# The w_down sums issued one step per store ahead of the FFN, and two modulation rows computed under the projections

## The chip, the cores and the metric

The kernel runs on one core of one Trainium2 chip. A core has a matrix engine (PE), a vector engine (DVE), an activation engine (ACT), a general engine (POOL), and a queue engine (SP) that mostly issues DMAs; POOL issues DMAs too. Each engine works through its own instructions strictly in order, and an instruction that waits for a semaphore holds everything behind it on that engine. The metric is the device time in microseconds (us) of one execution. Changes of this kernel under about 1% can't be told from no change.

## The reference

One layer of a hybrid block over 1024 tokens of width 1024, one sample, with 256 context tokens. Cut to what matters here:

```python
sh1, sc1, ga1, sh2, sc2, ga2 = split(silu(c) @ w_mod + b_mod)           # six modulation rows of 1024
hx = rmsnorm(x, g_pre_mix) * (1 + sc1) + sh1
u_pool, u_lru, u_gate, g_pool, g_lru = split(hx @ w_in)
y_pool = pool_mixer(u_pool)                    # 2D window means, grouped matmul
h_f, h_b = two RG-LRU scans over u_lru         # causal conv, gates, linear scan both ways
y_lru = (h_f + h_b) * gelu(u_gate)
m = sigmoid(g_pool) * (y_pool @ w_proj_pool) + sigmoid(g_lru) * (y_lru @ w_proj_lru)
x = x + ga1 * rmsnorm(m @ w_out, g_post_mix)
h = rmsnorm(x, g_pre_ffn) * (1 + sc2) + sh2
g, u = split(h @ w_up)                         # 2 x 3072 columns
f = (gelu(dwconv3x3(g)) * u) @ w_down
out = x + ga2 * rmsnorm(f, g_post_ffn)
```

## The kernel before, in words

Everything is in float32, but each matmul operand is split into a high and a low part in fp32r, and a product is three matmuls (high x high, high x low, low x high). So every weight tile of 128 x 1024 that comes from memory takes three steps, in `load_w` (L91): SP issues the load into a tile with the tag `raw`, ACT casts it to the high part (L89 CAST) and DVE subtracts for the low part (L89 TENSOR_TENSOR). The tag `raw` has three buffers for the whole kernel, given out in turn; who asks for the fourth waits until the first has been read. A unit of 48 matmuls of 128 x 512 (`unit_mm`, L228) makes 128 channels of a projection.

The stages, in order: a start (norm, the modulation of the first norm, up to about 100 us); z1 (to about 285 us: pooling, the gelu of the LRU's gate, gate units); z2, the LRU stage (to about 590 us: per channel block c one `lru_in` unit, four gate matmul groups, two scans on DVE, and a gate unit); pj, the projections (to 800 us: gate units that are left, `pp_unit` for y_pool, `pl_unit` for y_lru, and under them `form_pair`, which prepares three FFN weight sets and stores them in memory, and the loads of w_out); the w_out matmuls with the second norm (to 911 us); the FFN's up part (24 steps f, to 1401 us); the down part (to 1640 us).

The FFN and its down part use Strassen-like products, for which sums of blocks of w_down are needed. `sum_steps` (L850) forms them with accumulating DMAs on POOL's queue in a 128 x 2048 tile `n2raw` and stores them in `sd_d`: 12 blocks p of 5 steps, 60 steps of one to three DMAs, each step waiting for the one before it. They are issued three steps per f in the FFN loop (L972), chained behind the store of `gu_d` (L917).

The four later modulation rows (ga1, sh2, sc2, ga2) are computed by `mod_steps` (L252). For each row j there are eight loads `rawm` of w_mod, each with one DVE instruction that adds into `acc` (L264, L266); then four matmuls with a matrix of ones (`pm`, L270) that sum over partitions; then two row instructions on DVE (L273 with a row loaded into `rowb`, and for j=0, 2, 3 a second one, L275 to L279); then a store into `row_d`. `rawm` and `rowb` are both of the tag `raw`. Rows 0 and 1 are computed in z1, where weights are loaded three units ahead (L411); rows 2 and 3 in z2, three steps per channel block (L541). In pj and z2, `load_w` stands in the unit that uses the weight.

Tile tags in pj: `bc0` to `bc2` and `mq` are shared by stages, gate outputs and the pieces of `form_pair` (`piece`, L609, a ring of five). In the down part `finish` (L1029) loads a tile `xr` of x1 (two buffers), scales, adds and stores it; it is called for the second half of the tokens at product q=5 and for the first half at q=6, the last product.

The order on each engine comes from a scheduler: program order unless a `high_priority` offset or `issue_after` moves it.

Of the kernel before, what the change touches and what calls it, by code (L numbers as in the profile page):

```python
# [40 lines left out]
def block_kernel(ctx: ExitStack, tc: tile.TileContext, x, cx, vecs, rowv, icnt, w_mod1, w_mod, w_in, pool_w,  # L41
# [58 lines left out]
    n2raw = gpool.tile([P, 4, 512], F32, name="n2raw", tag="n2raw")  # L100
    epsc = cpool.tile([P, 1], F32, name="epsc")
# [150 lines left out]
    def mod_steps(zp, pp, rng, nbuf):  # L252
# [4 lines left out]
        for j in rng:  # L257
            acc = zp.tile([P, D], F32, name=uid("acc"), tag="acc", bufs=1)
# [9 lines left out]
            ps = pp.tile([P, SEQ], F32, name=uid("pm"), tag="pu", bufs=nbuf)  # L268
# [18 lines left out]
    with tc.tile_pool(name="z1", bufs=1, reuse_waits="tile") as zp:  # L287
        n_unit = [0]
        mods = mod_steps(zp, pp, (0, 1), 3)
# [3 lines left out]
        def gate_unit(which, c):  # L293
# [5 lines left out]
            G.dma_start(sg_d[c, :, which, :], s)  # L299
# [57 lines left out]
        def ug_unit(c):  # L357
# [6 lines left out]
            G.dma_start(gl_d[c], gl)  # L364
            return mm

        def pool_out(g, o, after):
# [16 lines left out]
            G.dma_start(yp_d[c], yp)  # L384
# [69 lines left out]
    with tc.tile_pool(name="z2", bufs=1, reuse_waits="tile") as zp, \  # L454
# [3 lines left out]
        def gate_unit(which, c):  # L458
# [6 lines left out]
            G.dma_start(sg_d[c, :, which, :], s)  # L465
# [22 lines left out]
        def lru_scan(c, xp, xc, wg):  # L488
# [46 lines left out]
            G.dma_start(yl_d[c], y)  # L535
# [18 lines left out]
    with tc.tile_pool(name="pj", bufs=1, reuse_waits="tile") as zp:  # L554
# [14 lines left out]
        for j, (which, c) in enumerate(gq):  # L569
# [5 lines left out]
            G.dma_start(sg_d[c, :, which, :], s)  # L575
# [20 lines left out]
        def pl_unit(c):  # L596
# [7 lines left out]
            G.dma_start(m_d[c], s)  # L604
# [4 lines left out]
        def piece():  # L609
            n_pc[0] += 1  # L610
            i = n_pc[0] % 5
# [41 lines left out]

        h2 = H("h2")
# [98 lines left out]
    with tc.tile_pool(name="ff", bufs=1, reuse_waits="tile") as zp:  # L753
# [96 lines left out]
        def sum_steps(p):  # L850
            n2v = n2raw.rearrange("p (g h) c -> p g h c", g=2)
            lo, up = w_down[p * P:(p + 1) * P, :], w_down[(NH + p) * P:(NH + p + 1) * P, :]
            hv = lambda a: a.rearrange("p (h c) -> p h c", h=2)
            add = lambda dst, src: G.dma_start(dst, src, accum_op=ALU.add)  # L854
            yield G.dma_start(n2v[:, 0], hv(lo)), G.dma_start(n2v[:, 1], hv(up))
            yield (add(n2v[:, 1], hv(lo)), add(n2v[:, 0, 0, :], lo[:, 512:1024]),
                   add(n2v[:, 0, 1, :], lo[:, 0:512]))
            yield add(n2v[:, 1, 0, :], lo[:, 512:1024]), add(n2v[:, 0, 0, :], up[:, 512:1024])
            yield add(n2v[:, 1, 0, :], up[:, 512:1024]),
# [299 lines left out]
```

## Time and profile before

| what | value |
|---|---|
| median of 3 runs | 1640.2 us (1632.53 to 1645.49) |
| the profiled execution's own time | 1641.79 us |
| span of the profiled execution | 1640.0 us |
| PE busy | 1568.3 us, 96% of the span |
| DVE busy | 1210.5 us, 74% |
| ACT busy | 687.0 us, 42% |
| POOL busy | 239.3 us, 15% |
| bytes moved by DMA | 289.15 MB, 176 GB/s over the span |

PE is busy nearly all the time, so the profile is read by looking for the places where PE stands idle and for what it waits there, and by asking for each stage how close another resource (a DMA, the three `raw` buffers, DVE) is to making PE wait. The view of stretches gives the busy time of each engine between two times, the clock that PE was granted (1.00 is full speed), the mean busy share of the DMA engines and the rate. In the view in order of time, "[3.79 <-ACT i L504]" says that the engine was idle for 3.79 us before the instruction and that an instruction of ACT, of line 504, ended it.

### The profile page before, as it was taken

How to read it: one execution, taken by the hardware profiler on the slowest of the kernel's cores; microseconds unless marked ns; L12 is line 12 of the kernel's file. 1: busy time of each engine (PE TensorE's matmuls, PEld its weight loads, DVE VectorE, ACT ScalarE, POOL GpSimd, SP SyncE). 2: the span in 40 equal slices, each digit the busy share in tenths (PEclk: the TensorE clock that was granted, in tenths of full speed). 3: DMA queues.
4: the chain of work that ended last, by engine and by line, in shares of the span. 5: the costliest groups of instructions: out<-in, count | busy, mean ns of one | idle time of the engine just before them, and what ended most of it. 6: DMA issues, size and time to landing. Idle time of an engine off the chain costs nothing.

```text
span 1640.0 us, 18320 instructions
## 1 busy us (share of the span) xinstructions
PE 1568.3 (96%) x6976; PEld 1265.2 (77%) x6976; DVE 1210.5 (74%) x1368; ACT 687.0 (42%) x828; POOL 239.3 (15%) x328
## 2 busy tenths in 40 slices
PE   6899999999999999999999989999899999999997
PEld 4588888877778788888788768877677777888885
DVE  7777664787887654354378889998798889787567
ACT  8523322565567734122143334333333334445442
POOL 1400200111112211010110122222222220000000
PEclk9999999999999999999999999999999999999999
DMA  8335454324233266399344567777667673687555
GB/s 314 114 103 165 138 184 139 127 97 148 84 103 116 90 232 230 124 289 300 131 141 142 209 195 186 193 199 197 176 183 180 178 187 110 217 320 256 175 188 192
DMA packets 98358, 289.15 MB, mean 176 GB/s; under 512 B 10871, under 2 KB 10999, under 8 KB 97502
## 3 DMA queue, kind: packets, MB, share of 16 engines
q1 hardware_dynamic: 60926, 170.64, 31.7%
q0 software_dynamic: 37344, 117.34, 24.2%
q8 instruction: 54, 0.88, 0.2%
q14 instruction: 34, 0.28, 0.1%
HBM read 221.34 MB, written 66.60 MB: 176 GB/s over the span
## 4 chain that ended last, share of the span: by engine, by line
PE 32%; DVE 10%; DMA 6%; ACT 2%; issue 2%; SPq 0%; DVEq 0%; ACTq 0%
PE pb L740 7%; PE pb L1017 6%; PE pb L706 5%; PE pc L740 4%; DMA raw<-in_w_up_dram 4%; PE pd L1017 4%; DVE gc L900 4%; PE pd L740 3%; PE pc L1017 2%; DVE wf L89 1%; DMA out_dram<-xr 1%; ACT wf L89 1%; DVE raw L801 0%; DMA xr<-x_d 0%; DVE w L89 0%
## 5 line engine op out<-in xcount | busy, mean ns | idle before, releaser
L242 PE MATMUL pu<-hx,whl 128*128 128x512 f32 x1056 | 266.7, 392 | 1.4 <-DVE whl L89 1.4
L900 DVE SCALAR_TENSOR_TENSOR gc<-gc,vec 128x945 f32<-128x945 f32 (+1 forms) x192 | 234.2, 1220 | 4.7 <-ACT gc L886 1.8
L89 ACT CAST whl<-raw 128x1024 fp32r<-128x1024 f32 (+1 forms) x109 | 109.1, 1003 | 305.8 <-DMA raw<-in_w_up_dram 74.4
L242 PEld LDWEIGHTS pu<-hx,whl 128*128 128x128 f32 x1056 | 186.8, 188 | 39.5 <-DVE whl L89 2.0
L89 DVE TENSOR_TENSOR whl<-raw,whl 128x1024 fp32r<-128x1024 f32 (+1 forms) x109 | 128.0, 1177 | 93.7 <-ACT whl L89 93.4
L242 PE MATMUL pg<-hx,whl 128*128 128x512 f32 x480 | 117.1, 396 | 0.0
L740 PE MATMUL pb<-h,wf 128*128 128x512 f32 x384 | 96.3, 400 | 11.3 <-ACT fk L810 11.3
L242 PEld LDWEIGHTS pg<-hx,whl 128*128 128x128 f32 x480 | 89.5, 191 | 19.3
L740 PEld LDWEIGHTS pb<-h,wf 128*128 128x128 f32 x384 | 71.8, 191 | 31.5 <-ACT fk L810 16.9
L740 PE MATMUL pb<-h,whl 128*128 128x512 f32 x384 | 94.9, 393 | 0.0
L706 PE MATMUL pb<-whl,mH 128*128 128x512 f32 x384 | 89.1, 392 | 1.0 <-ACT mH L700 1.0
L242 PE MATMUL pb<-hy,whl 128*128 128x512 f32 x384 | 87.8, 389 | 0.0
L706 PEld LDWEIGHTS pb<-whl,mH 128*128 128x128 f32 x384 | 71.5, 188 | 16.6 <-ACT mH L700 1.5
L740 PEld LDWEIGHTS pb<-h,whl 128*128 128x128 f32 x384 | 71.2, 188 | 16.9 <-ACT fk L810 2.5
L242 PEld LDWEIGHTS pb<-hy,whl 128*128 128x128 f32 x384 | 72.1, 188 | 14.9
L854 POOL DMA_DIRECT2D n2raw<-in_w_down_dram x72 | 63.0, 1006 | 122.9 <-DMA n2raw<-in_w_down_dram 122.6
L740 PE MATMUL pc<-nf,wf 128*128 128x512 f32 x288 | 72.9, 402 | 6.3 <-DVE gc L875 6.2
L1017 PE MATMUL pb<-hD 128*128 128x512 f32 x306 | 78.0, 390 | 0.0
L740 PEld LDWEIGHTS pc<-nf,wf 128*128 128x128 f32 x288 | 53.6, 190 | 22.5 <-DVE gc L875 11.5
L740 PE MATMUL pc<-nf,w 128*128 128x512 f32 x288 | 70.0, 391 | 0.2 <-DVE gc L847 0.2
L498 PE MATMUL pg<-xp,whl 128*128 128x512 f32 x192 | 61.3, 416 | 7.7 <-ACT i L504 7.6
L1017 PEld LDWEIGHTS pb<-hD 128*128 128x128 f32 x306 | 57.3, 188 | 12.3 <-DVE CA L1042 0.3
(319 smaller groups left out, 2986.9 us busy)
## 6 DMA issues: line engine op xcount, KB each, us to landing
raw<-in_w_up_dram SPq DMA_DIRECT2D x41, 512.0 KB, 4.6
raw<-in_w_in_dram SPq DMA_DIRECT2D x40, 512.0 KB, 4.7
n2raw<-in_w_down_dram POOLq DMA_DIRECT2D x36, 512.0 KB, 6.0
rawm<-in_w_mod_dram SPq DMA_DIRECT2D x32, 512.0 KB, 4.1
n2raw<-in_w_down_dram POOLq DMA_DIRECT2D x60, 256.0 KB, 5.7
rw<-gu_d SPq DMA_DIRECT2D x58, 256.0 KB, 5.1
gu_d<-gc POOLq DMA_DIRECT2D x24, 512.0 KB, 3.2
sd_d<-n2raw POOLq DMA_DIRECT2D x24, 512.0 KB, 4.6
```

Of the source, the lines that this page charges most:

```text
L89: return A.copy(hi, src), V.tensor_sub(lo, src, f32(hi))
L242: mm = T.matmul(ps[:, h * 512:(h + 1) * 512], wv[:, wi, k, :], act(h, k, ai), start=st, stop=sp)
L498: T.matmul(pg[:, h * 512:(h + 1) * 512], wg[:, wi, m, :], xp[:, ai, h * 512:(h + 1) * 512], start=(i == 0), stop=(i == 2))
L706: mm = T.matmul(ps[:, h * 512:(h + 1) * 512], mh[ai][:, k, :], wo[k][:, wi, h * 512:(h + 1) * 512], start=(k == 0 and i == 0), stop=(k == ...
L740: mm = T.matmul(ps, w(wi, j), b(ai, j), start=(start and j == 0 and i == 0), stop=(j == 3 and i == 2), skip_group_check=True)
L854: add = lambda dst, src: G.dma_start(dst, src, accum_op=ALU.add)
L900: V.scalar_tensor_tensor(o, gv[:, r0 + dr:r1 + dr, c0 + dc:c1 + dc], cw(i, j), o, op0=ALU.mult, op1=ALU.add)
L1017: T.matmul(bank[dst](t), op[:, gi, 512 + t * P:512 + (t + 1) * P], op[:, wi, H0], start=(first and p == 0 and i == 0), stop=(p == NH - 1 a ...
```

## The change

Three edits.

- `sum_steps` moves to the start of the kernel with a helper `sum_step`. One step is issued behind each store that POOL issues in z1 (18), z2 (16) and pj (11, the last behind `m_d` of c=4): 45 of the 60 steps, nine blocks p. The other 15 are issued one per f in the FFN, for f=2 to 16.
- Modulation rows 2 and 3 are computed in pj, three steps behind each `pl_unit` c=0 to 5, and no longer in z2. `acc` uses the tag `bc2`, so `piece` has a ring of four; the matmuls' result has the bank "c" of the projections.
- The four x1 tiles of the first half of the tokens are loaded at q=5 into the dead tile `N`, not in `finish`.

```diff
+    def sum_step(after, limit=45):
+        if n_step[0] >= limit:
+            return after
+        with tc.issue_after(after.ins):
+            i = next(dsteps[n_step[0]])[-1]
+        n_step[0] += 1
+        return i
...
-            G.dma_start(sg_d[c, :, which, :], s)
+            sum_step(G.dma_start(sg_d[c, :, which, :], s))
...
         gq = [(0, c) for c in range(6)] + [(1, c) for c in range(KT)]
-        mods = mod_steps(zp, pp, (2, 3), 2)
         cur = lru_in(0)
         for c in range(KT):
-            some(mods, 3)
             nxt = lru_in(c + 1) if c + 1 < KT else None
...
         def piece():
             n_pc[0] += 1
-            i = n_pc[0] % 5
+            i = n_pc[0] % 4
...
+        mods = mod_steps(lambda: zp.tile([P, D], F32, name=uid("acc"), tag="bc2"), lambda: pbank("c"), (2, 3))
         for c in range(KT):
             m_last = pl_unit(c)
+            some(mods, 3)
             if 2 <= c < 2 + NPF:
                 form_pair(c - 2)
...
-            for _ in range(3):
-                g = next(steps, None)
-                if g is not None:
-                    with tc.issue_after(chain[-1].ins):
-                        chain.append(next(g)[-1])
+            if f > 1:
+                chain.append(sum_step(chain[-1], 60))
...
+            xr = N[:, 0, 2 * t:2 * t + 2, :] if h == 0 else zp.tile([P, 2, 512], F32, name=uid("xr"), tag="xr", bufs=2)
+            if h:
+                load_x(xr, tt)
...
+            if q == 5:
+                for t in range(4):
+                    load_x(N[:, 0, 2 * t:2 * t + 2, :], t)
```

On PE, at the end of the projections, before: `pd`, `pc` with `yps` are the `pp_unit`s (six matmuls per input block), `pb` with `hy` the `pl_unit`s. Here is the `pl_unit` of c=2 with what follows it.

```order
L242 MATMUL pb_4909<-hy,whl_4906 128x512 x48
L242 MATMUL pc_4996<-yps_3967,whl_4993 128x512 x6
L242 MATMUL pc_4996<-yps_3972,whl_4993 128x512 x6
...
L242 MATMUL pb_5197<-hy,whl_5194 128x512 x48
L242 MATMUL pb_5304<-hy,whl_5301 128x512 x48
L242 MATMUL pb_5383<-hy,whl_5380 128x512 x48
```

And after, at the same place, with `pc_5003` and `pc_5436` the sums over partitions of rows 2 and 3.

```order
L265 MATMUL pb_4943<-hy,whl_4940 128x512 x48
L293 MATMUL pc_5003<-acc_4741,ones 128x512 x2
L265 MATMUL pc_5048<-yps_4025,whl_5045 128x512 x6
...
L265 MATMUL pb_5378<-hy,whl_5375 128x512 x48
L293 MATMUL pc_5436<-acc_5158,ones 128x512 x2
L265 MATMUL pb_5473<-hy,whl_5470 128x512 x48
```

The row sum now stands behind `pl_unit` c=2 (`pb_4943`) and ahead of `pp_unit` c=6 (`pc_5048`), and the second one between `pl_unit`s c=5 and c=6.

On SP, the loads around `pl_unit` c=2 before: the two FFN weight tiles of the first `form_pair`, then the weights of `pp_unit` c=6 and `pl_unit` c=3.

```order
L618 DMA raw584_4961<-in_w_up_dram 128x1024
L619 DMA raw585_4962<-in_w_up_dram 128x1024
L585 DMA sgp568_4729<-sg_d_78 128x1024
L585 DMA sgp572_4786<-sg_d_78 128x1024
L94 DMA raw592_4991<-in_w_pp_dram 128x1024
L94 DMA raw596_5048<-in_w_pl_dram 128x1024
```

After, the same place, and then the place around `pl_unit` c=5 (`raw642_5468` is the weight of `pl_unit` c=6). All tiles named `raw`, `rawm` and `rowb` share the three buffers.

```order
L284 DMA rawm567_4997<-in_w_mod_dram 128x1024
L284 DMA rawm568_5000<-in_w_mod_dram 128x1024
L278 DMA rowb570_5006<-in_rowv_dram 1x1024
L278 DMA rowb571_5009<-in_rowv_dram 1x1024
L607 DMA sgp548_4751<-sg_d_78 128x1024
L607 DMA sgp552_4808<-sg_d_78 128x1024
L640 DMA raw572_5013<-in_w_up_dram 128x1024
L607 DMA sgp559_4879<-sg_d_78 128x1024
L607 DMA sgp563_4936<-sg_d_78 128x1024
L607 DMA sgp579_5041<-sg_d_78 128x1024
L641 DMA raw573_5014<-in_w_up_dram 128x1024
L94 DMA raw580_5043<-in_w_pp_dram 128x1024
```

```order
L278 DMA rowb631_5439<-in_rowv_dram 1x1024
L278 DMA rowb632_5442<-in_rowv_dram 1x1024
L94 DMA raw633_5446<-in_w_out_dram 128x1024
L607 DMA sgp641_5466<-sg_d_78 128x1024
L94 DMA raw635_5451<-in_w_out_dram 128x1024
L607 DMA sgp645_5525<-sg_d_78 128x1024
L94 DMA raw637_5456<-in_w_out_dram 128x1024
L94 DMA raw639_5461<-in_w_out_dram 128x1024
L94 DMA raw642_5468<-in_w_pl_dram 128x1024
```

Two `rowb` loads now take two of the three buffers ahead of `raw573_5014` and `raw580_5043`; in the second place they stand ahead of three w_out loads and of `raw642_5468`. The second `rowb` (`rowb571_5009`) and `raw580_5043` have the same buffer, and so do `raw635_5451` and `raw642_5468`.

On POOL, in the FFN, before, and then after: `gu_d` is the store of a finished f, `n2raw` and `sd_d` are the sums.

```order
L917 DMA gu_d_6389<-gc806_6629 128x1024
L854 DMA n2raw_86<-in_w_down_dram 128x1024
L854 DMA n2raw_86<-in_w_down_dram 128x512 x5
L917 DMA gu_d_6389<-gc815_6748 128x1024
L860 DMA sd_d_85<-n2raw_86 128x1024 x2
L855 DMA n2raw_86<-in_w_down_dram 128x1024 x2
L854 DMA n2raw_86<-in_w_down_dram 128x512 x2
```

```order
L929 DMA gu_d_6479<-gc806_6707 128x1024
L106 DMA n2raw_86<-in_w_down_dram 128x1024 x2
L929 DMA gu_d_6479<-gc815_6822 128x1024
L105 DMA n2raw_86<-in_w_down_dram 128x1024
L105 DMA n2raw_86<-in_w_down_dram 128x512 x2
L929 DMA gu_d_6479<-gc824_6949 128x1024
```

Between two stores of `gu_d` there were three steps, and there is one.

## Rows read from the trace of the kernel before

**Rows 1.** Stretches: length, busy us (instructions) by engine, PE clock, DMA share, GB/s.

```profile
300.00:400.00 100.00, 95.34 (x443) 77.08 (x442) 78.69 (x68) 64.12 (x64) 15.21 (x10) 0.97 0.34 108
400.00:500.00 100.00, 95.59 (x446) 76.88 (x445) 84.92 (x70) 62.64 (x62) 19.78 (x13) 0.98 0.35 113
...
900.00:1000.00 100.00, 89.45 (x372) 69.91 (x371) 86.47 (x96) 36.12 (x45) 18.55 (x29) 0.97 0.63 192
1000.00:1100.00 100.00, 99.80 (x434) 79.98 (x433) 94.87 (x99) 37.89 (x45) 25.67 (x36) 1.00 0.77 204
1100.00:1200.00 100.00, 93.44 (x393) 74.12 (x392) 83.69 (x88) 36.86 (x45) 23.22 (x33) 0.97 0.68 182
```

**Rows 2.** Longest wait of PE, 300 to 560 us (total us, times, longest).

```profile
PE pg L498 <- ACT i L504: 7.6, 2, 3.8
```

**Rows 3.** In order of time, ACT, LRU stage (start, length; idle before).

```profile
385.90 1.04 ACT L89 CAST whl<-raw 128x1024 fp32r<-128x1024 f32 x1 [4.22 <-DMA raw<-in_w_in_dram]
```

**Rows 4.** In order of time, SP, LRU stage.

```profile
363.63 0.33 SPq L94 DMA_DIRECT2D raw<-in_w_in_dram  x1
364.88 11.72 SPq L261 DMA_DIRECT2D rawm<-in_w_mod_dram  x3
...
379.61 0.33 SPq L94 DMA_DIRECT2D raw<-in_w_in_dram  x1
```

**Rows 5.** Longest waits of PE in the FFN (total us, times, longest).

```profile
PE pb L740 <- ACT fk L810: 11.3, 8, 2.8
PE pd L740 <- ACT fk L810: 6.2, 2, 5.2
```

**Rows 6.** Longest wait of ACT in the FFN.

```profile
ACT whl L89 <- DMA raw<-in_w_up_dram: 68.6, 18, 11.1
```

**Rows 7.** The chain that ended last, one transfer in the FFN (start, length).

```profile
1156.28 8.49 DMA raw<-in_w_up_dram
```

**Rows 8.** In order of time, ACT, FFN.

```profile
1164.84 1.04 ACT L89 CAST whl<-raw 128x1024 fp32r<-128x1024 f32 x1 [11.09 <-DMA raw<-in_w_up_dram]
```

**Rows 9.** In order of time, DVE, end.

```profile
1629.96 1.28 DVE L1049 SCALAR_TENSOR_TENSOR xr<-CA,rs,xr 128x1024 f32<-128x1024 f32 x1 [2.34 <-DMA xr<-x_d]
1631.16 0.68 DVE L1042 TENSOR_TENSOR CA<-pc,CA 128x512 f32<-128x512 f32 x1
...
1635.55 1.42 DVE L1049 SCALAR_TENSOR_TENSOR xr<-CA,rs,xr 128x512 f32<-128x512 f32 x2 [0.94 <-DMA xr<-x_d]
```

**Rows 10.** Projections by stretches, PE alone: length, busy, clock, DMA share, GB/s.

```profile
562.00:690.00 128.00, 128.00 (x567) 1.00 0.53 185
690.00:740.00 50.00, 50.00 (x222) 1.00 0.92 293
```

**Rows 11.** In order of time, PE, a row sum in the LRU stage, a unit of the projections.

```profile
358.59 1.88 PE L270 MATMUL pm<-acc,ones 128*128 128x512 f32 x4
...
722.79 11.04 PE L242 MATMUL pc<-yps,whl 128*128 128x512 f32 x48
```

**Rows 12.** In order of time, DVE, row instructions of row 2 in z2.

```profile
362.40 1.21 DVE L273 TENSOR_TENSOR acc<-pm,rowb 1x1024 f32<-1x1024 f32 x1
363.64 1.21 DVE L277 SCALAR_TENSOR_TENSOR acc<-acc,rowb 1x1024 f32<-1x1024 f32 x1
```

**Rows 13.** Groups of DVE and ACT in the projections (busy, mean ns).

```profile
L89 DVE TENSOR_TENSOR whl<-raw,whl 128x1024 fp32r<-128x1024 f32 x28 | 34.2, 1221 | 30.5 <-ACT whl L89 30.4
...
L602 DVE SCALAR_TENSOR_TENSOR sgp<-sgp,pb 128x1024 f32<-128x1024 f32 x7 | 8.5, 1220 | 39.6 <-PE pb L242 32.6 <-DMA sgp<-sg_d 7.0
```

**Rows 14.** The same view, ACT.

```profile
L89 ACT CAST whl<-raw 128x1024 fp32r<-128x1024 f32 x28 | 29.4, 1051 | 78.1 <-PE pb L242 30.4 <-PE pd L242 22.4 <-DMA raw<-in_w_out_dram 12.7
```

**Rows 15.** DMA issues, 600 to 690 us: count, KB, median us to landing.

```profile
raw<-in_w_pp_dram SPq DMA_DIRECT2D x5, 512.0 KB, 4.0
```

**Rows 16.** DMA issues, 690 to 740 us.

```profile
raw<-in_w_pp_dram SPq DMA_DIRECT2D x2, 512.0 KB, 7.5
```

More of the change, by code (lines that the diff above doesn't have):

```diff
@@ L100, in block_kernel, with sum_steps @@
     n2raw = gpool.tile([P, 4, 512], F32, name="n2raw", tag="n2raw")
+    def sum_steps(p):
+        n2v = n2raw.rearrange("p (g h) c -> p g h c", g=2)
+        lo, up = w_down[p * P:(p + 1) * P, :], w_down[(NH + p) * P:(NH + p + 1) * P, :]
+        hv = lambda a: a.rearrange("p (h c) -> p h c", h=2)
+        add = lambda dst, src: G.dma_start(dst, src, accum_op=ALU.add)
+        yield G.dma_start(n2v[:, 0], hv(lo)), G.dma_start(n2v[:, 1], hv(up))
+        yield (add(n2v[:, 1], hv(lo)), add(n2v[:, 0, 0, :], lo[:, 512:1024]),
+               add(n2v[:, 0, 1, :], lo[:, 0:512]))
+        yield add(n2v[:, 1, 0, :], lo[:, 512:1024]), add(n2v[:, 0, 0, :], up[:, 512:1024])
+        yield add(n2v[:, 1, 0, :], up[:, 512:1024]),
+        yield tuple(G.dma_start(sd_d[p, i], n2v[:, i].rearrange("p h c -> p (h c)")) for i in range(2))
+    dsteps = [st_ for p in range(NH) for st_ in [sum_steps(p)] * 5]
+    n_step = [0]
+    def sum_step(after, limit=45):
[5 more added lines that the diff above has]
+        return i
     epsc = cpool.tile([P, 1], F32, name="epsc")
@@ L257, in mod_steps @@
         for j in rng:
-            acc = zp.tile([P, D], F32, name=uid("acc"), tag="acc", bufs=1)
+            acc = new_acc()
             for k in range(KT):
@@ L267, in mod_steps @@
                 yield
-            ps = pp.tile([P, SEQ], F32, name=uid("pm"), tag="pu", bufs=nbuf)
+            ps = new_ps()
             for h in range(2):
@@ L288, in block_kernel @@
         n_unit = [0]
-        mods = mod_steps(zp, pp, (0, 1), 3)
+        mods = mod_steps(lambda: zp.tile([P, D], F32, name=uid("acc"), tag="acc", bufs=1),
+                         lambda: pp.tile([P, SEQ], F32, name=uid("pm"), tag="pu", bufs=3), (0, 1))
         wload = lambda u: wq.pop(0)
@@ L464, in gate_unit @@
                 A.activation(s, ps, AF.Tanh, scale=0.5)
-            G.dma_start(sg_d[c, :, which, :], s)
+            sum_step(G.dma_start(sg_d[c, :, which, :], s))
         LC = SEQ
@@ L534, in lru_scan @@
             V.tensor_mul(y, y, gl)
-            G.dma_start(yl_d[c], y)
+            sum_step(G.dma_start(yl_d[c], y))
         gq = [(0, c) for c in range(6)] + [(1, c) for c in range(KT)]
-        mods = mod_steps(zp, pp, (2, 3), 2)
         cur = lru_in(0)
         for c in range(KT):
-            some(mods, 3)
             nxt = lru_in(c + 1) if c + 1 < KT else None
@@ L574, in block_kernel @@
             A.activation(s, ps, AF.Tanh, scale=0.5)
-            G.dma_start(sg_d[c, :, which, :], s)
+            sum_step(G.dma_start(sg_d[c, :, which, :], s))
         hy = H("hy")
@@ L603, in pl_unit @@
             V.tensor_add(s, s, mp)
-            G.dma_start(m_d[c], s)
+            sum_step(G.dma_start(m_d[c], s))
             return s
@@ L652, in block_kernel @@
         ga1g, B2, S2 = bcs
+        assert n_step[0] == 45
         h2 = H("h2")
@@ L848, in mid @@
             st[f] = (gc, u2)
[L850 to L859, printed above, removed]
-            yield tuple(G.dma_start(sd_d[p, i], n2v[:, i].rearrange("p h c -> p (h c)")) for i in range(2))
-        steps = iter([st_ for p in range(NH) for st_ in [sum_steps(p)] * 5])
         chain = []
@@ L1027, in block_kernel, with load_x @@
         EPRI = 150
+        def load_x(xr, tt):
+            nc.sync.dma_start(xr, x1_d[tt * P:(tt + 1) * P, :].rearrange("p (h c) -> p h c", h=2))
         def finish(h, t):
             tt = 4 * h + t
-            xr = zp.tile([P, 2, 512], F32, name=uid("xr"), tag="xr", bufs=2)
-            nc.sync.dma_start(xr, x1_d[tt * P:(tt + 1) * P, :].rearrange("p (h c) -> p h c", h=2))
+            xr = N[:, 0, 2 * t:2 * t + 2, :] if h == 0 else zp.tile([P, 2, 512], F32, name=uid("xr"), tag="xr", bufs=2)
+            if h:
+                load_x(xr, tt)
             ss = small.tile([P, 1], F32, name=uid("ss"), tag="ss1", bufs=3)
```

6 lines of the change are left out of this document (3 added, 3 removed).

## The prediction

> **What bounds the kernel now.** I read the page first, for the busy shares: PE has work for 1568.3 of 1640.0 us, so about 70 us are to be had, and only where PE stands idle. Then the view of stretches, to find where that is [rows 1]. Two stretches in the LRU stage have PE at 95.34 and 95.59 of 100 us, so 9.1 us of idle time. In the FFN the stretches 900 to 1000 and 1100 to 1200 have 10.6 and 6.6 us, while 1000 to 1100, with the sums running too, has 0.2. In the projections there is none: PE is busy 128.00 of 128.00 us and 50.00 of 50.00 [rows 10]. Then the list of waits, for what ended the idle times, and the view in order of time around the longest. Each edit touches one of these places, so the sum has a term for each.
>
> **The LRU stage (modulation rows 2 and 3 leave it).** PE waited 7.6 us for ACT's gate instructions of L504 in two gaps of 3.8 [rows 2]. ACT had not been slow: ahead of L504 it stood 4.22 us at the cast of a w_in tile whose load had not landed [rows 3]. That load was issued late, at 379.61, because SP stood in the `rawm` group before it, 11.72 us for three issues [rows 4]: all three `raw` buffers were taken by the modulation. Without the modulation these loads are limited by the units alone. So the 9.1 us of idle time go, nearly whole. After a gap PE runs for a while at half clock; the two stretches show 0.97 and 0.98 granted [rows 1], which is 2 to 3 us of full clock withheld in each, part of it while PE stood anyway. I take 3 us for both. **Gain 12** (9 to 14).
>
> **The FFN (three of four sum steps leave it).** PE waited 11.3 + 6.2 = 17.5 us for ACT's copies `fk` [rows 5]. They are short; they stood behind casts of `w_up` tiles, for which ACT waited 68.6 us in 18 places, the longest 11.1 [rows 6]. The longest is the pattern: a w_up load took 8.49 us [rows 7], the cast behind it stood 11.09 [rows 8], and PE's longest wait, 5.2, is at the copy queued behind that cast [rows 5]. An unhurried load of the same size takes 4.0 us [rows 15]. With the clock (0.97 in two stretches [rows 1], about 5 us over the stage net of idle time) the waits cost 22.5. Of 60 steps 45 leave, so I take three quarters: **gain 16**. Lower end 6, if only the longest wait and its clock go; upper end 26, if the loads' delay goes whole and some of DVE's with it.
>
> The Trainium skill has a rule that bears on this, in "DMA: Bandwidth & Descriptors", section "Issuing engines are not separate DMA queues": DMAs issued by different engines run on the same 16 DMA engines and interleave. By it a load on SP's queue slows when POOL's sums run beside it, as the 8.49 us load shows; by it too the traffic that leaves the FFN slows the loads where it goes. A rule of separate queues would make both terms zero.
>
> **The end (x1 loaded early).** DVE stands 2.34 us at L1049 for the `xr` of the tile ahead, and L1042 of the last tile starts at 1631.16, right behind it; then the last L1049 stands 0.94 us for its own `xr` [rows 9]. With the tiles there, both waits go, as far as PE has finished the last product by then. **Gain 3** (2 to 4).
>
> **The sums in z1, z2 and pj.** The issues stand on POOL. In z1 the instructions behind them on POOL (fills of borders, stores) are waited for by nobody soon, and weights are asked for three units ahead, so I cost them at nothing; the cover there is one unit, 11 us [rows 11], against loads of 4.0 to 7.5 [rows 15, 16]. In z2 a2 (L514) stands on POOL behind `yl_d` and the step, a delay of up to 2 us in some channel blocks, before a Sqrt that waits for the second direction anyway: nothing, at most 2 us. In pj they add DMA traffic, below.
>
> **The projections (the modulation rows arrive): the costly part.** The matmuls and DVE instructions themselves move and cost the same in both places: 2 x 1.88 us of PE [rows 11]. What is new is that the modulation stands among `load_w`s that are asked for by the unit that uses them. The stage had one unit per weight (11.04 us [rows 11]) and no gap; where the first `form_pair`s ran, DMA was already at 0.92 and 293 GB/s [rows 10], and a w_pp load took 7.5 us there, not 4.0 [rows 15, 16].
>
> *First place, behind `pl_unit` c=2.* Two `rowb` loads take two of the three buffers. They come free when DVE has done L296 and L300, which need the row sum on PE, which stands behind the unit. The same hold is visible in z2: SP's next issues, at 363.63 and 364.88 [rows 4], are 0.03 us behind the ends of L273 (362.40 + 1.21) and L277 (363.64 + 1.21) [rows 12]. In z2 and z1 it cost PE little; here the load that is held, by `rowb571_5009`'s buffer, is the weight of the very next unit, `pp_unit` c=6. From the end of `pl_unit` c=2: gate and sum 1.22 + 1.22 [rows 13], the row instructions 1.21 + 1.21 [rows 12], the load 5.5 (between 4.0 and 7.5; nearer the low end since the held queue has let the others drain), the cast 1.05 [rows 14], the subtraction 1.22 [rows 13]: 12.6. PE has the row sum, 1.9, to do in it. Idle 10.7 (9 to 12.7).
>
> *Second place, ahead of `pl_unit` c=5.* From there on 20 loads of 512 KB go through three buffers before that unit's weight is in (two for `pp_unit`s, three for `pl_unit`s, six `rawm`, five `w_up`, four `w_out`), where 14 would without `rawm`. In that time PE has 12.6 + 4 x 11 = 56.6 us of idle time and work. One buffer carries nine of the loads in a row, seven with cast and subtraction (2.3) and two with one DVE instruction (1.3 each): 5 + 9 x load + 18.7, so 60 us at 4.0, 73 at 5.5, 91 at 7.5. By bytes: about 10.5 MB of these loads, 2 of `sgp`, 6 of stores of `form_pair`, 1 of `m_d`, 1.6 of sums, 21 MB, at 293 GB/s [rows 10] 72 us. I take 70, idle 14 (3 to 34).
>
> The Trainium skill, same page, section "Specifications", gives about 358 GB/s as the limit of memory for one core; by that figure, an estimate, the 21 MB would take 59 us and the idle time would be 3 at most and the whole sum 11 less. The stretch with 0.92 share moved 293 [rows 10], and no run here shows more over 50 us.
>
> *Third place, behind `pl_unit` c=5.* `raw642_5468`, the weight of `pl_unit` c=6, has the buffer of `raw635_5451`, a w_out tile, whose own load waits for the tile ahead to be split, and that split stands on DVE behind the gate of `pl_unit` c=5. So after this unit: gate 1.2 and split 1.2, a load 4.0 to 5.5 and a split 2.3, then again a load and 2.3: 15 to 18, of which 1.9 is the row sum. Idle 13 to 16; I take 13.
>
> After each of the three PE is at half clock for a while, 2 to 3 us as in the LRU stage [rows 1]; I take 2.4 each, 7. **Cost 10.7 + 14 + 13 + 7 = 45** (31 to 72).
>
> **The sum.** The profiled execution took 1641.8 us, 1.6 above the median of the three runs. 1641.8 - 12 - 16 - 3 + 45 = 1655.8; against the median 1654.
>
> **The rivals.**
>
> *The projections' holes stay small: faster.* If the second and third weight land in their unit's time, only the first place costs, 10.7 + 2.4 = 13, and the time is 1640 - 31 + 13 = 1622. For it: in z2 the same hold [rows 4, 12] is not where PE's idle time was [rows 2]. Against it: there the held load was not the next unit's. It decides when PE's idle time between 690 and 820 us is below about 15.
>
> *The projections become bound by DMA: slower.* If the loads take 7.5 us throughout [rows 16], the second place costs 34 and the third 18: 1654 + 20 + 5 = 1679. For it: the stretch is at 0.92 before anything is added [rows 10]. The Trainium skill's rule on shared DMA engines, above, speaks for it. Against it: the bytes alone give 72 us, not 91.
>
> *The FFN does not gain: slower.* DVE was busy 94.87 of 100 us where PE had no gap [rows 1]. If the FFN is bound by DVE once the loads are early, the idle time returns as waits for DVE's `gc`, the gain is 3, not 16, and the time 1667. For it: DVE is at 84 to 95 in all three stretches. Against it: PE and DVE are both below full in the stretches with gaps, so neither bounds those.
>
> **How the numbers follow.** The forecast, holes of 33 to 50 us against a gain of 25 to 35, has a chance of 0.55, with its own range 1640 to 1666. Faster by the first rival 0.13. Slower by the second 0.20, by the third 0.12. 1% is 16.4 us, about what a measurement of this kernel can tell from no change: below 1624 is faster, above 1656.6 slower. The forecast lies just below the upper border, so 0.08 of its chance falls above: faster 0.13, same 0.47, slower 0.40. The range leaves out 0.1 on each side: 1627 to 1674.
>
> **What would show it.** Right: PE has three idle times in the projections, of 9 to 13 us behind `pc_5003`, 3 to 34 ahead of `pl_unit` c=5, 13 to 16 behind `pc_5436`, each ended by the split of a weight; the LRU stage has no gap over 2 us; w_up loads in the FFN take 4 to 5 us; the last L1049 does not wait. Wrong: PE without a gap between 690 and 820 us, or an FFN stage as long as before (490 us).

## The result, and the profile after

The changed kernel takes 1685.8 us (median of 4 runs), the kernel before 1642.9 beside it: a ratio of 1.027, 95% interval 1.022 to 1.032. The prediction was 1654 with a range to 1674. So the kernel got slower, as the sum said, but the time lies outside the range.

The profiled execution took 1687.21 us, its span is 1685.4. Cut into stages by the first matmul of each in the view in order of time, against the kernel before:

| stage | before, us | after, us | difference | forecast |
|---|---|---|---|---|
| start and z1, to the first gate matmul of the LRU | 307.4 | 313.7 | +6.3 | 0 |
| LRU stage and gate units, to the first `pp_unit` | 317.4 | 315.5 | -1.9 | -16 (12, and the row matmuls that leave) |
| `pp_unit` c=0 to 3 | 43.5 | 53.6 | +10.1 | 0 |
| `pl_unit`s, to the first w_out matmul | 131.8 | 185.7 | +54.0 | +49 (45, and the row matmuls) |
| w_out and second norm | 111.7 | 111.7 | 0 | 0 |
| FFN, up part | 488.5 | 468.3 | -20.2 | -16 |
| down part | 228.3 | 228.4 | +0.1 | 0 |
| after the last matmul | 11.3 | 8.4 | -2.9 | -3 |

The projections, the FFN and the end came out close to the forecast. The three stages ahead of them did not: 6.3 + 14.1 + 10.1 = 30.5 us are lost there against the forecast, and that is nearly the whole error. (The table compares two single traces. Over all traces of this document, the FFN with three steps per f, as before, takes 481 to 491 us, and the tail without the early x1 loads 9.1 to 11.3.) The stretches that answer to [rows 1] and [rows 10] (length, busy us and instructions of PE, of its weight loads, of DVE, ACT and POOL, granted clock, DMA share, GB/s):

```profile
100.00:200.00 100.00, 95.20 (x416) 78.61 (x415) 63.19 (x67) 30.54 (x40) 24.98 (x46) 0.97 0.66 190
300.00:400.00 100.00, 100.00 (x485) 82.37 (x484) 75.51 (x65) 68.04 (x69) 21.91 (x18) 1.00 0.36 110
600.00:700.00 100.00, 87.14 (x365) 71.15 (x365) 44.82 (x38) 30.35 (x30) 18.13 (x30) 0.91 0.76 245
...
800.00:900.00 100.00, 71.00 (x285) 56.51 (x286) 45.74 (x58) 21.95 (x30) 11.65 (x17) 0.83 0.56 195
...
1200.00:1300.00 100.00, 99.12 (x431) 79.97 (x430) 93.70 (x97) 36.94 (x46) 10.18 (x15) 1.00 0.43 124
```

PE is full in 300 to 400, where it had 4.7 us of idle time [rows 1]; it is at 71 of 100 us in 800 to 900, at a granted clock of 0.83. In the stretch of the FFN shown the DMA share is 0.43 and DVE is at 93.70 with PE at 99.12.

The three holes foreseen in the projections, in order of time, PE; each row is the first matmul after the hole, the hole in brackets:

```profile
752.20 4.21 PE L265 MATMUL pc<-yps,whl 128*128 128x512 f32 x9 [13.04 <-ACT whl L89]
...
814.11 2.50 PE L265 MATMUL pb<-hy,whl 128*128 128x512 f32 x5 [16.01 <-ACT whl L89]
...
842.85 3.35 PE L265 MATMUL pb<-hy,whl 128*128 128x512 f32 x7 [14.00 <-ACT whl L89]
```

They stand at the places named, ended by a weight's cast, at 13.0, 16.0 and 14.0 us against 10.7, 14 and 13. The nine matmuls behind the first take 4.21 us, 0.47 each, twice the 0.23 of a full-speed unit [rows 11]. The first hole's chain, DVE and then SP and ACT:

```profile
737.48 1.22 DVE L624 SCALAR_TENSOR_TENSOR sgp<-sgp,pb 128x1024 f32<-128x1024 f32 x1 [9.66 <-PE pb L265]
738.73 1.22 DVE L625 TENSOR_TENSOR sgp<-sgp,sgp 128x1024 f32<-128x1024 f32 x1
739.87 1.20 DVE L296 TENSOR_TENSOR acc<-pc,rowb 1x1024 f32<-1x1024 f32 x1
741.11 1.21 DVE L300 SCALAR_TENSOR_TENSOR acc<-acc,rowb 1x1024 f32<-1x1024 f32 x1
```

```profile
741.11 0.33 SPq L641 DMA_DIRECT2D raw<-in_w_up_dram  x1
742.35 0.37 SPq L94 DMA_DIRECT2D raw<-in_w_pp_dram  x1
```

```profile
751.10 1.04 ACT L89 CAST whl<-raw 128x1024 fp32r<-128x1024 f32 x1 [2.60 <-DMA raw<-in_w_pp_dram]
```

SP issues the w_up load at the end of L296 (739.87 + 1.20) and the w_pp load, the weight of the next unit, 0.03 us behind the end of L300. Two sizes in it were wrong and partly cancel: the load took 8.7 us, not 5.5, and PE starts at the end of the cast, without the subtraction. In the run with the move of the modulation alone (below) the same load took 6.5 us and the hole was 10.8; in the changed kernel POOL issued two transfers of a sum 1.5 us ahead of the load:

```profile
740.80 1.78 POOL L105 DMA_DIRECT2D n2raw<-in_w_down_dram  x2
```

The end, DVE: the last L1062 (L1049 before, [rows 9]) waits no more.

```profile
1681.62 0.74 DVE L1062 SCALAR_TENSOR_TENSOR N<-CA,rs,N 128x512 f32<-128x512 f32 x1
```

In the FFN, the waits of PE that answer to [rows 5], 7.8 us where there were 17.5, and of ACT for w_up ([rows 6], 68.6):

```profile
PE pb L765 <- ACT fk L835: 5.6, 8, 1.3
PE pd L765 <- ACT fk L835: 2.2, 4, 1.0
```

```profile
ACT whl L89 <- DMA raw<-in_w_up_dram: 49.8, 10, 6.9
```

And what was not foreseen. In z1 there is one hole. It lies in the stretch 100 to 200, the first of the list above, which before the change had PE nearly full and a DMA share of 0.42, not 0.66:

```profile
100.00:200.00 100.00, 99.71 (x447) 82.11 (x446) 68.92 (x71) 33.32 (x43) 14.45 (x33) 1.00 0.42 140
```

PE waits there 4.80 us for the context tiles `xs`, which DVE scales. DVE stood 4.03 us for a `rawm` of the modulation, then worked without a pause up to that scaling; before the change it had stood 1.78 us at the same place. The row of PE names a cast on ACT that ended at the same moment; the scaling of `xs` ended 0.15 us before PE went on. In order of time PE and DVE after, DVE before:

```profile
173.89 1.94 PE L166 MATMUL pt<-ident,xs 128*128 128x128 f32 x8 [4.80 <-ACT whl L89]
```

```profile
164.63 1.28 DVE L289 SCALAR_TENSOR_TENSOR acc<-rawm,cs,acc 128x1024 f32<-128x1024 f32 x1 [4.03 <-DMA rawm<-in_w_mod_dram]
```

```profile
160.89 1.28 DVE L266 SCALAR_TENSOR_TENSOR acc<-rawm,cs,acc 128x1024 f32<-128x1024 f32 x1 [1.78 <-DMA rawm<-in_w_mod_dram]
```

A hole in the LRU stage, in order of time, POOL, DVE, PE:

```profile
524.24 0.55 POOL L111 DMA_DIRECT2D sd_d<-n2raw  x1 [5.00 <-DMA n2raw<-in_w_down_dram]
524.80 2.34 POOL L538 TENSOR_TENSOR a<-r 128x1280 f32<-128x1280 f32 x1
```

```profile
527.17 1.49 DVE L539 SCALAR_TENSOR_TENSOR th<-a,th 128x1280 f32<-128x1280 f32 x1 [3.80 <-POOL a L538]
534.12 1.48 DVE L89 TENSOR_TENSOR xp<-xc,xp 128x1280 fp32r<-128x1280 f32 x1
```

```profile
535.65 1.22 PE L522 MATMUL pg<-xp,whl 128*128 128x512 f32 x2 [5.70 <-DVE xp L89]
```

The store of a sum stands on POOL and waits 5.00 us for the sum's transfer; a2 (`a` in the row of L538) stands behind it, DVE behind a2, and the split of xp, for which PE waits, behind that on DVE. A second hole of this stage, at a gate unit, POOL, ACT and PE:

```profile
595.76 0.86 POOL L105 DMA_DIRECT2D n2raw<-in_w_down_dram  x1 [7.96 <-DMA n2raw<-in_w_down_dram]
596.33 1.41 POOL L588 DMA_DIRECT2D st<-yp_d  x2
```

```profile
600.66 1.05 ACT L89 CAST yps<-st 128x1024 fp32r<-128x1024 f32 x1 [16.38 <-DMA st<-yp_d]
```

```profile
616.63 3.70 PE L265 MATMUL pb<-hx,whl 128*128 128x512 f32 x8 [5.54 <-ACT whl L89]
```

A sum's wait of 7.96 us stands ahead of loads of yp, and the cast of the gate unit's weight stands on ACT behind the casts of yp. And one in the `pp_unit`s, POOL, ACT and PE:

```profile
649.68 0.53 POOL L111 DMA_DIRECT2D sd_d<-n2raw  x1 [5.88 <-DMA n2raw<-in_w_down_dram]
650.20 1.06 POOL L601 DMA_DIRECT2D st<-yl_d  x2
```

```profile
655.28 1.05 ACT L89 CAST hy<-st 128x1024 fp32r<-128x1024 f32 x1 [7.28 <-DMA st<-yl_d]
```

```profile
669.37 10.95 PE L265 MATMUL pd<-yps,whl 128*128 128x512 f32 x36 [7.33 <-DVE sgp L615]
```

Here a sum's wait holds the loads of yl, whose splits then stand on ACT and DVE ahead of what the `pp_unit`s need. Additions of the moved modulation stand there on DVE, too; the runs below tell the two apart (8 of the 10 us come with the sums alone, none with the modulation alone).

### The profile page after: what moved, and what is told of

Its sections match the earlier page's. It is cut to its first block, busy times and chain, and to the rows that moved or that the text cites. A ratio compares the mean times of both kernels' runs of the same rounds, so it can differ in the third digit from the quotient of the medians.

```text
span 1685.4 us, 18315 instructions
## 1 busy us (share of the span) xinstructions
PE 1572.7 (93%) x6976; PEld 1270.4 (75%) x6976; DVE 1222.4 (73%) x1368; ACT 683.5 (41%) x828; POOL 238.8 (14%) x328
## 5 line engine op out<-in xcount | busy, mean ns | idle before, releaser
L89 DVE TENSOR_TENSOR whl<-raw,whl 128x1024 fp32r<-128x1024 f32 (+1 forms) x109 | 136.1, 1251 | 65.1 <-ACT whl L89 64.7
L265 PE MATMUL pb<-hy,whl 128*128 128x512 f32 x384 | 93.1, 404 | 30.0 <-ACT whl L89 30.0
L731 PEld LDWEIGHTS pb<-whl,mH 128*128 128x128 f32 x384 | 71.5, 188 | 16.5 <-ACT mH L725 1.3
L929 POOL DMA_DIRECT2D gu_d<-gc x24 | 13.1, 547 | 433.8 <-DVE gc L925 433.8
L289 DVE SCALAR_TENSOR_TENSOR acc<-rawm,cs,acc 128x1024 f32<-128x1024 f32 x28 | 35.9, 1284 | 45.9 <-DMA rawm<-in_w_mod_dram 45.8
```

Source lines behind the costliest of these rows:

```text
L89: return A.copy(hi, src), V.tensor_sub(lo, src, f32(hi))
L265: mm = T.matmul(ps[:, h * 512:(h + 1) * 512], wv[:, wi, k, :], act(h, k, ai), start=st, stop=sp)
L289: V.scalar_tensor_tensor(acc, raw, cs[:, k, 0:1], acc, op0=ALU.mult, op1=ALU.add)
L731: mm = T.matmul(ps[:, h * 512:(h + 1) * 512], mh[ai][:, k, :], wo[k][:, wi, h * 512:(h + 1) * 512], start=(k == 0 and i == 0), stop=(k == ...
L929: chain.append(G.dma_start(gu_d[f], gc[:, 1, :]))
```

## The experiments

All times beside runs of the kernel before on the same chip, as a ratio with its 95% interval.

### The parts one at a time

**The sums alone.** The diff of the change without `mods` in pj, with `piece` as before, and without `load_x`.

> The kernel before with the sums' edit alone (modulation rows 2 and 3 stay in the LRU stage, x1 is loaded as before). Theory, each edit costs where the trace of the changed kernel shows it and the parts add up: the FFN's up part 20 us shorter, z1 7 longer, the LRU stage about 14 longer (POOL holds a2 behind a sum step that waits for its DMA), the first projections about 10 longer (POOL holds the loads of yp and yl): 1642 - 20 + 7 + 14 + 10 = 1653. Rival, the sums harm only together with the moved modulation: 1642 - 20 = 1622, and no gap of PE over 4 us between 100 and 700 us beyond the two of the LRU stage before.

Measured: 1660.6 us, ratio 1.012 (1.010 to 1.015). The FFN takes 465.7 us, 23 less; z1 291.3, the LRU stage 339.8, the pp units 51.9: 15, 22 and 8 more. (Here and below z1 is counted without the start, from the first matmul that reads `hx`: 276.6 before, 283.8 in the changed kernel.) The rival falls: the sums harm by themselves, by 45 us gross against a gain of 23. The theory's 11 us net were too few.

**The modulation's move alone.**

```diff
-        mods = mod_steps(zp, pp, (2, 3), 2)       # in z2, with some(mods, 3)
+        mods = mod_steps(..., lambda: pbank("c"), (2, 3))   # in pj
+            some(mods, 3)                          # behind each pl_unit
```

> The kernel before with the move of modulation rows 2 and 3 alone (sums in the FFN as before). Theory, the three holes of PE in the projections come from the order of the raw buffers: they stay, near 13, 16 and 14 us, the stretch from the first pl unit to the first w_out matmul is about 54 us longer than before, the LRU stage 16 shorter (row matmuls included): 1642 + 38 = 1680. Rival, the holes come from the sums' traffic under the projections: the holes shrink below 5 us each and the time is 1642 - 16 + 15 = 1641 or less.

Measured: 1668.0, ratio 1.017 (1.015 to 1.019). The LRU stage takes 299.0 us, 18 less, with no gap over 2 us; the stretch of the pl units 182.5, 51 more. The waits of PE in 690 to 830 us (total, times, longest):

```profile
PE pb L265 <- ACT whl L89: 29.0, 2, 15.1
PE pc L265 <- ACT whl L89: 10.8, 1, 10.8
```

The holes are there without any sums, at 10.8, 15.1 and 13.8: the rival falls. The time is 12 below the expectation: the LRU stage gained 2 more and the holes were 3 smaller, the FFN took 482.8 us with the code of before (488.5 in the trace before), and the kernel before was 2 faster beside it.

**The early x1 loads alone.**

> The kernel before with the early x1 loads alone. Theory: the tail after the last matmul is 3 us shorter, 1639. Rival, four more loads at product 5 delay the weights of the last product and give it back: 1642.

Measured: 1638.5, ratio 0.999 (0.997 to 1.001). The tail after the last matmul is 8.4 us where it was 11.3, as in the change; in the time it can't be told from nothing.

The three ratios together, 1.2 + 1.7 - 0.1 = 2.8%, make the change's 2.7%: the parts add in the whole. By stage they don't: z1 loses 15 us with the sums alone and 7 in the change, and the sums cost the LRU stage 22 us alone and 16.5 in the change (315.5, against 299.0 with the move alone).

### The holes in the projections

**The row tiles out of the raw buffers.** As the move alone, and

```diff
-            t = gpool.tile([1, D], F32, name=uid("rowb"), tag="raw", bufs=3)
+            t = n2raw[0:1, o:o + 2, :].rearrange("p a b -> p (a b)")     # o = 0 or 2
```

> As the move of the modulation alone, but its row tiles are loaded into n2raw, which is idle there, and take no raw buffer. Theory, the hold by the row tiles makes the first hole and a part of the third: the first hole falls from 13 to under 3 us, the third from 14 to 5 to 10, the second stays at 10 to 16; 18 to 24 us less than with the row tiles in the ring, 1658. Rival, the holes are the DMA's rate and not the order: all three stay within 3 us and the time is 1680.

Measured: 1652.0, ratio 1.007 (1.005 to 1.009), 16 less than the move alone. The first hole is gone, the third is 4.1 (13.8 with the move alone), the second stays at 15.1:

```profile
PE pb L265 <- ACT whl L89: 19.2, 2, 15.1
```

So the row tiles made the first hole, as in the prediction's first place, and not the second. They made most of the third, too. The prediction's working of the third place names a w_out tile's buffer and not the row tiles that the w_out loads stand behind.

**All of the modulation's loads out of the raw buffers.** `rawm` and `rowb` alternate between two halves of `n2raw`; places and bytes as in the move.

```diff
+        def mod_raw(i):
+            n_mr[0] += 1
+            o = 2 * (n_mr[0] % 2)
+            t = n2raw[:, o:o + 2, :] if i is None else n2raw[0:1, o:o + 2, :]
+            return t.rearrange("p a b -> p (a b)")
```

> The move of the modulation alone, at the same places as in the change, but all its loads (rawm and the row tiles) go through two halves of n2raw and none through the raw ring; the bytes are the same. Theory, the second hole of 15 us is the turnaround of three raw buffers: it falls under 5 us, as does the third, and the time is 1642 - 18 + 4 + 5 = 1633. Rival, it is the rate of the DMA engines, which have the same bytes to move: the second hole stays at 12 us or more and the time at 1648 to 1652, as with the row tiles alone out of the ring.

Measured: 1633.1, ratio 0.995 (0.993 to 0.997). The second hole falls from 15.1 to 1.3 us, and the third is 4.8:

```profile
PE pb L265 <- ACT whl L89: 6.1, 2, 4.8
```

The same bytes move in all three runs. The 60 us up to the end of the second hole, with the move alone, with the row tiles out, and with all loads out:

```profile
720.00:780.00 60.00, 44.88 (x191) 36.73 (x189) 36.56 (x43) 15.43 (x20) 9.91 (x15) 0.87 0.96 314
```

```profile
705.00:765.00 60.00, 45.53 (x197) 36.64 (x196) 36.57 (x40) 12.60 (x17) 8.20 (x13) 0.90 0.78 261
```

```profile
690.00:750.00 60.00, 59.18 (x257) 47.81 (x256) 37.30 (x40) 13.37 (x17) 7.96 (x13) 1.00 0.92 302
```

The hole does not follow the rate of the DMA engines: it is 15.1 us at a share of 0.78, and 1.3 at 0.92. It follows the buffers, of which the modulation here has two of its own beside the three, so that loads start earlier. In 675 to 735 us the DMA engines are at 0.95 and 312 GB/s here, at 0.53 and 175 with the move alone:

```profile
675.00:735.00 60.00, 60.00 (x263) 48.81 (x262) 29.98 (x34) 12.30 (x16) 8.82 (x14) 1.00 0.95 312
```

So the second hole comes from the turnaround of three buffers, and the rival falls as the cause. That the nearly full engines add to the hole where the ring has put the loads off, as with the move alone (0.96), is not ruled out.

**The modulation earlier, under the gate and first pp units.** `acc` and the row tiles in `n2raw`, `rawm` in the raw buffers, two steps behind each unit; early x1 loads.

> Sums in the FFN as before, early x1 loads as in the change, and modulation rows 2 and 3 in the projections, but earlier: two steps behind each gate unit and each of the first pp units, ahead of form_pair, with acc and the row tiles in n2raw. Theory, the move costs nothing where the raw ring is not short: LRU stage 299 (317 before), no gap over 3 us in the projections, row matmuls 4 us there: 1642 - 18 + 4 - 2 = 1626. Rival, these units load yp and yl too and ACT and DVE are behind: gaps of 10 to 15 us, 1640.

Measured: 1645.2, ratio 1.002 (0.999 to 1.005): a miss. The holes of the projections are gone (131.8 us, as before), but the LRU stage with the gate units takes 322.6, and there:

```profile
PE pc L293 <- ACT sg L599: 10.3, 1, 10.3
PE pg L522 <- DVE xp L89: 5.2, 1, 5.2
```

The row matmul waits for the bank of a gate unit whose activation is late on ACT. Whether the 5.2 us at xp come from this edit was not tried.

**Through n2raw, with the early x1 loads; and the same with earlier steps.**

> The move of the modulation with all its loads through n2raw, and the early x1 loads; the sums stay in the FFN as before. Theory, both gains add: 1633 - 2 = 1631, tail 8.4 us. Rival, the early x1 loads give nothing in the time: 1633.

Measured: 1631.3, ratio 0.993 (0.991 to 0.996), tail 8.4.

```diff
         for c in range(4):
             pp_unit(c)
+            some(mods, 2)
         for c in range(KT):
             m_last = pl_unit(c)
-            some(mods, 3)
+            some(mods, 2)      # and two behind each pp_unit of this loop
```

> As the run before it, but the modulation has two steps behind each unit from the first pp unit on, so that it is nearly done before form_pair begins. Theory, what is left of the holes (6 us with the clock behind them) comes from the loads under form_pair: the stretch of the pl units falls from 145.6 to 137, and the time to 1624. Rival, the loads of yl and the bank of the row matmuls are in the way there: a new gap of 4 us or more, 1630 or more.

Measured: 1627.4, ratio 0.992 (0.990 to 0.994). The pl units take 142.8 us against 143.3 in the run before it: the holes under `form_pair` are gone, but the rival's gap is there, `pc` waiting for DVE's L296:

```profile
PE pc L265 <- DVE acc L296: 4.7, 1, 4.7
```

The gain over the run before it can't be told from nothing.

**The row matmuls in bank "d".**

> As the early modulation with its loads through n2raw and the early x1 loads, but the row matmuls write the bank of the pp unit after next, not that of the next one. Theory: PE's gap of 4.7 us behind the first row matmuls was the next pp unit waiting for DVE to read that bank; it goes, with 2 us of clock: 1627 - 6 = 1621. Rival, it was the bank's order with the pl units and another unit waits instead: 1627.

Measured: 1633.3, ratio 0.995 (0.992 to 0.997): a miss. The wait for L296 is gone, and three smaller ones stand in its place:

```profile
PE pb L740 <- ACT mH L734: 3.1, 1, 3.1
PE pb L265 <- DVE sgp L624: 2.3, 1, 2.3
PE pd L293 <- DVE sgp L615: 1.6, 1, 1.6
```

They sum to 7.0 against 5.7 with bank "c" (the 4.7 above and one of 1.0). So other units wait instead, as the rival says.

### The cost of the sums ahead of the FFN

**45 steps left out.**

> The kernel before with 45 of the 60 sum steps left out altogether (the down part reads the sums of the first three blocks for all twelve); the other 15 as in the change, one per f. It shows what the FFN gains where nothing is paid elsewhere. Theory: FFN 466 us as in the change, 22 less, 1640 - 20 = 1620. Rival, the FFN is bound by DVE: less than 5 us gained, 1636.

Measured: 1619.7, ratio 0.988 (0.983 to 0.993), FFN 467.6 us. The FFN's gain, 21 us, is what the change also gets; DVE doesn't take it back.

**The LRU stage's steps behind a2.** In z2, no step behind the stores, and

```diff
-                G.tensor_mul(a2, r, r)
+                am = G.tensor_mul(a2, r, r)
+                if d == 1:
+                    sum_step(sum_step(am))
```

> The sums alone, but in the LRU stage both steps of a channel block stand behind the second a2 of the scan, so that no a2 stands on POOL behind a step that waits for a transfer; the number of steps is the same. Theory, POOL's order costs the LRU stage: DVE's wait for a2 falls from 40 to under 30 us as before the change, the stage is 10 to 15 us shorter than with the sums alone (339.8), and the time 1660 - 12 = 1648. Rival, the sums' traffic slows the w_in loads and that makes the gaps: the stage stays at 335 or more and the time at 1657 to 1662.

Measured: 1648.0, ratio 1.005 (1.003 to 1.007), 12.7 less than the sums alone. DVE's wait for a2, 300 to 640 us, with the sums alone and then in this run (28.9 before the change):

```profile
DVE th L539 <- POOL a L538: 40.2, 10, 5.8
```

```profile
DVE th L541 <- POOL a L538: 30.9, 12, 5.0
```

The LRU stage is 10 us shorter (329.8), and the pp units take 43.5 again. POOL's order is one cause in the LRU stage. It is not the only one: 12 us are left there, and z1 is at 291.3 as before this edit.

**A quarter of the bytes.** As with the steps behind a2, each early transfer 128 of 512 columns wide.

> The sums alone with the steps of the LRU stage behind a2, and each transfer of the 45 early steps cut to a quarter of its columns (the same issues and waits; the down part reads three of the complete blocks for all). Theory, what is left of the cost there is the sums' traffic, which slows the w_in loads and the context loads: z1 falls from 291.3 to 280 or less, the LRU stage from 329.8 to 322 or less, the time from 1648 to 1626. Rival, the issues on POOL cost it: 1642 or more.

Measured: 1626.0, ratio 0.992 (0.989 to 0.995). z1 takes 280.3 and the LRU stage 321.0, 11 and 9 us less, with the same issues and the same order on POOL. So most of what was left is traffic, or the waits on POOL that grow with it. The w_in loads of 140 to 300 us (median us to landing at the row's end; the trace has the landing of three of the nine), with the sums alone, with a quarter of the bytes, and before:

```profile
raw<-in_w_in_dram SPq DMA_DIRECT2D x9, 512.0 KB, 10.3
```

```profile
raw<-in_w_in_dram SPq DMA_DIRECT2D x9, 512.0 KB, 7.5
```

```profile
raw<-in_w_in_dram SPq DMA_DIRECT2D x9, 512.0 KB, 6.9
```

In the changed kernel the four w_in loads of this stretch whose landing shows took 3.5 to 4.4 us, with all of the bytes. So the slow w_in loads are a part of the loss with the sums alone (z1 + 15), and not of the one in the changed kernel (z1 + 7). With the sums alone ACT stands for such a load in the LRU stage, too:

```profile
400.86 1.04 ACT L89 CAST whl<-raw 128x1024 fp32r<-128x1024 f32 x1 [7.33 <-DMA raw<-in_w_in_dram]
```

**No steps in the projections.** 30 steps ahead of the FFN, two per f in it.

> The sums alone, with 30 steps ahead of the FFN (18 in z1, 12 in the LRU stage), none in the projections, and 30 in the FFN, two per f. Theory, in the projections the steps hold POOL's loads of yp and yl: without them the four pp units take 43.5 us as before (51.9 with the sums) and the gap of 9 us at the gate units goes, 18 less; the FFN, with half of the steps, gives back a third of its gain of 23, 7 more: 1660 - 18 + 7 = 1649. Rival, the loads of yp and yl are slow by traffic and not by POOL's order: 1660 + 7 = 1667.

Measured: 1664.6, ratio 1.013 (1.010 to 1.017), near the rival's number but not for its reason. The pp units take 43.5 us, as the theory said. The gap at the gate units is still there (8.0 us), so it doesn't come from the steps in the projections. And the FFN takes 482.4: with two steps per f it gives back 17 of its 23 us, not 7. That is in the range of the traces with three steps, 481 to 491; with one it takes 466 to 469.

**The steps of the projections behind the pl units.**

> The sums alone, with the steps of the projections moved from the gate units' stores to those of the pl units, two each: the same number of steps, none on POOL ahead of the loads of yp and yl. Theory, POOL's hold of these loads costs the pp units: 43.5 us (51.9 with the sums), the pl units 133 to 138, 1660 - 8 = 1652. Rival, it is traffic or the late LRU stage: the pp units stay at 50 or more and the time at 1658 or more.

Measured: 1669.2, ratio 1.018 (1.012 to 1.023). The pp units take 43.5, as with POOL's hold of the loads as the cause, but the pl units take 145.5, 12 more than with the sums alone: the steps hold other things there, and the time missed the expectation by 17. That the run with the steps behind a2 has the hold and yet 43.5 is not settled; there the LRU stage ends in another order.

### A version that beats both

Early modulation through `n2raw` in bank "d", early x1 loads, and 40 sum steps ahead of the FFN: 16 in z1, 24 in the LRU stage behind a2, none in the projections; 20 in the FFN, one per f.

```diff
+                if d == 1:
+                    for _ in range(3):
+                        am = sum_step(am, 40)
...
-            for _ in range(3):
-                chain.append(sum_step(chain[-1], 60))
+            chain.append(sum_step(chain[-1], 60))
```

> As the run with bank d, and with sums ahead of the FFN where they were cheapest: 16 steps in z1, 24 in the LRU stage behind a2 (three per channel block, now without modulation loads), none in the projections, 20 in the FFN, one per f. Theory: z1 7 to 14 longer by traffic, the LRU stage 5 to 10 longer, the FFN 16 shorter: 1621 + 3, 1615 to 1630. Rival, with the modulation gone the LRU stage has room for the traffic: z1 +7, LRU +2, 1614.

Measured: 1623.8, ratio 0.989 (0.985 to 0.993). z1 takes 281.9 us, 5 more than before; the LRU stage 300.6, 1.7 more than without sums; the FFN 468.7. The stretches of the LRU stage:

```profile
300.00:400.00 100.00, 100.00 (x485) 82.41 (x484) 76.18 (x65) 68.28 (x69) 27.71 (x24) 1.00 0.45 121
400.00:500.00 100.00, 100.00 (x483) 82.05 (x482) 87.12 (x68) 69.10 (x68) 33.14 (x33) 1.00 0.57 160
```

Sixteen steps cost 22 us there with the modulation's loads beside them and a2 behind them, 12 with the steps behind a2, and 16.5 in the changed kernel, without the modulation but with a2 behind them; now, without the modulation, behind a2 and with no steps in the projections, 24 steps cost 2. That is the rival's case for this stage: PE is full at a DMA share of 0.45 to 0.57. The version is faster than the kernel before by 1.1% (0.7 to 1.5) and than the changed one by 3.7% (medians of 1623.8 and 1685.8, from different runs). It can't be told from the early modulation in bank "c" (0.992), which has the sums in the FFN.

## Why the prediction was wrong

**The step that failed** is "The sums in z1, z2 and pj", costed at nothing; it cost 30.5 us.

In z1 the prediction counted the weights, which are asked for three units ahead, and POOL's own instructions. The hole of the changed kernel, 4.80 us with PE at a granted clock of 0.97 in its stretch, is at other loads that came late beside the sums' traffic, a `rawm` and the context tiles: 6.3 us. The w_in loads do not explain it there (3.5 to 4.4 us), as they do in part with the sums alone (10.3, near the cover of 11).

In the LRU stage the delay of a2 was put at "up to 2 us", the issue time of a step; a step also waits for the transfer of the step before it, 5.00 us in the row shown, and a2 waits behind. In pj the same waits hold the loads of yp and yl on POOL, which the prediction didn't look at: it named DMA traffic alone there. The hold of yp shows in the LRU stage's second hole (14.1 us for the stage), that of yl in the `pp_unit`s (10.1 us). How much of these is POOL's order and how much the traffic is settled for the sums alone only in part: behind a2 the LRU stage is 10 us shorter, at a quarter of the bytes 9 more.

Together 6.3 + 14.1 + 10.1 = 30.5 us. With these 1655.8 + 30.5 = 1686 against 1687.2 of the profiled execution; the other terms miss by 5 (projections) and -4 (FFN). Of the signs that the prediction named, the three holes and the last L1062 (its L1049) came as it said, and the w_up loads were a little shorter than that (a median of 3.5 us); "no gap over 2 us" in the LRU stage did not (5.7).

**The LRU stage**: the mechanism was right (299.0 us and no gap over 2 us with the move alone); the gain of 14.6, without the row matmuls, then went to the sums in the same stage.

**The FFN**: right in cause and nearly in size, 20 against 16. The share, three quarters of the steps for three quarters of the waits, does not hold in form: with half of the steps gone 6 of the 23 us were gained in the one trace of it, no more than such traces differ.

**The projections**: places and cause right, 54.0 against 48.8 with the row matmuls: holes 13.0 + 16.0 + 14.0 = 43.0, row matmuls 3.8, clock about 7. That the first place came out at 10.8 without the sums, against 10.7, is partly luck: two wrong sizes cancel in it. In the second place the ring is the cause. The byte count beside it (21 MB at 293 GB/s) gave nearly the same number, and the engines are full in the changed kernel in the 60 us up to this hole:

```profile
755.00:815.00 60.00, 43.99 (x189) 36.03 (x188) 35.75 (x41) 14.72 (x19) 10.75 (x16) 0.87 0.99 320
```

But the runs show the hole at a share of 0.78, too, and the same bytes without a hole, so the count doesn't give its cause; and the 293 GB/s were no limit, since 302 to 320 over 60 us were seen. The estimate that the prediction drew from the Trainium skill's page "DMA: Bandwidth & Descriptors", section "Specifications" (at its limit of about 358 GB/s for one core an idle time of 3 us at most) fails: the hole was 16.0 us. No row shown here reaches that rate.

**The rivals**: the second (bound by DMA) gave 1679, near the result, by a cause that the runs with loads taken out of the ring rule out; the projections alone would have had to lose 25 us more than the forecast by it, and they lost 5. The third (DVE bounds the FFN) is ruled out by the FFN's gain. The rule of the Trainium skill's page "DMA: Bandwidth & Descriptors", section "Issuing engines are not separate DMA queues", agrees with the runs: a quarter of the sums' bytes, on POOL's queue, brought SP's loads in z1 from 10.3 back to 7.5 us. The prediction applied it to the projections and not to z1 and the LRU stage.

## What to carry to other kernels

Work moved out of a stage that waits for loads must be costed where it lands in three ways: its bytes against the cover of the loads there, its buffers against the ring that the unit's own weights go through, and its waits against what stands behind them on the issuing engine's queue. A chain of transfers issued on an engine that also computes belongs behind the instruction that others wait for, not ahead of it; here that was worth 12.7 us. And a small row tile in a weight ring takes a whole buffer until a late reduction has read it: here two such tiles at a time made a hole of 10.8 us and most of another.

## What the runs showed of the hardware

The FFN's length does not go in proportion with the number of sum steps in it: three steps per f 481 to 491 us in the traces, two 482 in one trace, one 466 to 469. And in the run through `n2raw`, PE was full for the 60 us from 675 to 735 at a DMA share of 0.95 and 312 GB/s: nearly full DMA engines did it no harm where loads had buffers to start early.
